# Attention's output projection as seven products over both token halves, with sums made by accumulating transfers

## The chip, the core and the metric

One core of a Trainium2 chip runs the kernel in one launch. TensorE (PE) multiplies, with its own queue for loading weights (PEld); VectorE (DVE), ScalarE (ACT) and GpSimd (POOL) work on elements; SyncE (SP) issues transfers, and so can POOL. Sixteen DMA engines carry the transfers of all queues. The metric is device time in microseconds; a run is compared by the median of several executions.

## The reference, cut to what matters

Two layers over 1024 tokens of width 1024, in fp32. Layer 0 mixes tokens by sliding-window attention (16 query heads, 4 key heads, blocks of 128, a sink per head), layer 1 by a gated recurrence; after each follows an MLP with squared ReLU (1024 to 4096 to 1024). The part that the change touches:

```python
def sliding_window_attention(h, positions, w_qkv, b_qkv, sinks, w_o):
    ...
    out = jnp.einsum('bnkgqs,bnskd->bnqkgd', probs.astype(vb.dtype), vb)
    return out.reshape(bsz, seq, Q_DIM) @ w_o

def sqrelu_mlp(h, w_up, w_down):
    return jnp.square(jax.nn.relu(h @ w_up)) @ w_down

    for layer in range(DEPTH):
        h = rmsnorm(x, mix_norm[layer])
        y = ...                       # attention in layer 0, recurrence in layer 1
        x = x + y
        h = rmsnorm(x, mlp_norm[layer])
        x = x + sqrelu_mlp(h, mlp_w_up[layer], mlp_w_down[layer])
```

## The kernel before, in words

All activations lie transposed: a tile is 128 channels by 512 tokens, so the width is 8 tiles (`KT`) and the tokens are two halves (`NH`). To keep fp32 accuracy, every operand of a matmul is split into a rounded high part and a rest (`split` for tokens, `weight_split` for weights: a cast on ACT, a subtraction on DVE), and `mm3` makes three matmuls of 128x512 for one product: high by high, high by low, low by high.

Most large products are already made by Strassen's method in Winograd's form: the operands are cut in two by two (inner channels and output channels of the weights; inner channels and token halves of the activations), and seven products with operand sums take the place of eight. The numbers 1 to 7 in the code name these products. In the MLPs, `begin` makes the operands that need the first token half only (1 and 2), `finish` the sums for 5, 3, 6, 7 and 4; `pair_first` starts the first two output tiles with products 1 and 2 while the sums are made, and `pair` does the rest.

Attention's output projection (`o_proj`) is plain: for each token half and each of 8 output tiles it sums 8 inner tiles. `attention` interleaves three stretches: `attend` of the first half beside `qkv` of the second, `attend` of the second half beside `o_proj` of the first, and `o_proj` of the second half beside `mlp_first`. `attend` works through 16 blocks a half (`attend_block`: scores, a masked maximum that includes the sink's column, exponentials, transposes; `values`: the product with the values).

The code states operations with a modelled cost in program order (`Schedule.add`). A planner (`forward`, `backward`, four passes) then lays them on the engines by readiness and due time, gives tiles their buffers, and fixes one order for each engine; PE takes them by their rank, the others by how late they may be. Each queue runs strictly in that order on the chip. All operations are issued from one helper, so nearly all rows of the profile have one line, and tiles are told apart by their tags: `a` (60 buffers of operands and activations), `t` (18), `m` (6), `wr` (raw weights), `wh` and `wl` (split weights), `p` and `q` (4 PSUM banks each), `c` (constants), `d` (kept in HBM).

A plain transfer is issued by SP (`dma`). `dma_sum` loads one tile on SP and adds a second onto it by an accumulating transfer on POOL's queue; before, the down projections' weights of product 5 are made so.

Of the kernel before, what the change touches and what calls it, by code (L numbers as in the profile page):

```python
# [139 lines left out]
SUM = 6000.0  # L140
# [242 lines left out]
class Net:  # L383
# [156 lines left out]
    def split(self, src, new=None):  # L540
        hi, lo = ((new or self.a)(F32R) for _ in range(2))
        self.copy(hi, src, TH, psum=False)
        self.tt("any", lo, src, hi.bitcast(F32), ALU.subtract)
        return hi, lo
# [46 lines left out]
    def lay_out(self):  # L591

        for v in (self.par, self.ones, self.ident, self.prev_mask, self.mean, self.eps, self.neg, *self.square[:1]):
            v.buf.handle()
# [52 lines left out]
    def gained(self, which, kt, hf):  # L647

        u = self.t()
        self.act(u, self.x[kt][hf], AF.Copy, scale=self.gain(which, kt))  # L650
        return u
# [7 lines left out]
    def begin(self, which):  # L659

        self.b, self.u = {k: [] for k in range(1, 8)}, []
        for kt in range(KT):
            u = self.gained(which, kt, 0)
            self.b[1 + kt // HK].append(self.split(u))
            self.u.append(self.keep(u))
            yield

    def finish(self, which, upper_first=False, keep=False):

        x, t, q01, q11 = self.b, [], [], []  # L670
        self.u3, self.u5 = [], []

        def stored(j):
            z = self.t()
            self.dma(z, self.u[j], 4 * P * TH)
            return z

        def lower():
            for j in range(HK):
                q01.append(self.gained(which, j, 1))  # L680
                t.append(stored(j))
                self.tt("any", t[j], q01[j], t[j], ALU.subtract)
                x[5].append(self.split(t[j]))
                if keep:
                    self.u5.append(self.keep(t[j]))
# [7 lines left out]

        for part in (upper, lower) if upper_first else (lower, upper):
            part()
        for j in range(HK):
            self.tt("any", t[j], q11[j], t[j], ALU.subtract)
            x[6].append(self.split(t[j]))
        for j in range(HK):
            self.tt("any", q01[j], q11[j], q01[j], ALU.subtract)  # L700
            x[7].append(self.split(q01[j]))
        self.u4 = []
        for j in range(HK):
            z = stored(j + HK)
            self.tt("any", z, z, t[j], ALU.subtract)
            x[4].append(self.split(z))
            if keep:
                self.u4.append(self.keep(z))
        return x

    def mlp_first(self, layer):
        self.layer, self.hid, self.y = layer, {}, {}
        yield from self.begin(2 + layer)
        if not layer:
            self.weigh(0)

    def mlp_second(self):
        self.first = [self.pair_first(m) for m in range(FIRSTS[self.layer])]
        x = self.finish(2 + self.layer, keep=True)
        if not self.layer:  # L720
            self.weigh(1)
# [42 lines left out]
    def inner_operands(self, own, kept, homes, stream=False):  # L764
# [15 lines left out]
        def split(name, z):  # L780
            y = self.split(z, new if homes else self.t)
# [16 lines left out]
        for j, c in enumerate((L, R) if homes else ()):  # L798
            hi, lo = part(own[j], R, "R")
            self.copy(hi, t[0][:, c], 2 * P, psum=False)  # L800
            self.tt("any", lo, t[0][:, c], hi.bitcast(F32), ALU.subtract, 2 * P)
# [176 lines left out]
    def mlp(self, cut):  # L978

        x = self.mlp_second()  # L980
        for m in range(MT // 2):
            if m == INNER[self.layer]:
                homes = iter(HOMES)
                self.quarters = {2: self.inner_operands(self.b[2], self.u[HK:], homes),
                                 3: self.inner_operands(self.b[3], self.u3, None),
# [4 lines left out]
            if self.layer and m == 1:  # L990
# [9 lines left out]
    def operands(self, name, p, T, S, held=False):  # L1000
# [11 lines left out]
        elif name == 5:  # L1012
# [3 lines left out]
            self.dma_sum(w, *(self.io["down"][self.layer, k, p, :, 1] for k in range(2)), 4 * P * TH)  # L1016
# [126 lines left out]
    def rope_tables(self):  # L1143
# [3 lines left out]
        late = self.x[KT // 2][0]  # L1147
        posf, ang = self.const((P, n)), self.const((P, n))
# [144 lines left out]
    def first_loads(self):  # L1293
# [4 lines left out]
        self.op("ACT", self.nc.scalar.dma_start, [self.par], [self.io["par"]], 100, self.par, self.io["par"], tail=3000.0)  # L1298
        for kt in range(KT):
# [64 lines left out]
    def attend(self, hf, out):  # L1364

        blocks = range(hf * BPH, hf * BPH + BPH)
        for gp in range(NG // 2):
# [3 lines left out]
            for e in range(2):  # L1371
                g = 2 * gp + e
                for j in range(2):
                    out[g, j] = self.a()
                for n in blocks[::4]:
# [4 lines left out]
                    self.values(g, n, parts, out)  # L1380

    def values(self, g, n, parts, out):
# [690 lines left out]
```

## Time and profile before

| | |
|---|---|
| median of 3 runs | 2018.03 us (2015.84 to 2018.79) |
| the profiled execution | 2015.63 us, span 2013.9 us |
| PE busy | 2003.4 us, granted clock 0.999 |
| DVE, ACT, POOL busy | 1801.6, 1308.0, 70.7 us |
| transfers | 521.25 MB, 75.1% of the DMA engines' time on SP's queue, 2.3% on POOL's |

The page is of one profiled execution, the sums of the prediction are made against its own time. Busy time of PE includes the overlap of pipelined matmuls, so a matmul's price is read from how many fit into a stretch, not from the duration of one. A line of the list of waits says which engine waited on which tile for whom, how long in all, how often, and the longest. A group of instructions shows engine, operation, result <- operands by tags, shapes, count, busy time and the mean of one, then the idle time ahead of them.

### The profile page before, as it was taken

To read this page: it belongs to the slowest core of one execution; us is meant where nothing else is said; L and a number is where in the kernel's file an instruction comes from. 1 tells how busy PE (TensorE), PEld (TensorE's weight loads), DVE (VectorE), ACT (ScalarE), POOL (GpSimd) and SP (SyncE) were. 2 spreads that over 40 slices of the span, in tenths; PEclk is the share of its full clock that TensorE was granted. 3 is DMA by queue.
4 is the path that set the end of the run, shared out by engine and by line. 5 is a ranking of instruction groups with operands and counts; after the bars stand their busy time and mean duration, and the time that the engine had idled before them with its cause. 6 is when DMAs were issued, how large, how long until landed. Compare 5 with 4: busy or idle time off the path is not lost. (4 is left out here: it accounts for less than half of the span.)

```text
span 2013.9 us, 40072 instructions
## 1 busy us (share of the span) xinstructions
PE 2003.4 (99%) x13820; PEld 1700.7 (84%) x13820; DVE 1801.6 (89%) x3636; ACT 1308.0 (65%) x2746; POOL 70.7 (4%) x161
## 2 busy tenths in 40 slices
PE   9999999999999999999999999999999999999998
PEld 8887888899998888888888888888889998888887
DVE  8879879899898979889999999999999998987985
ACT  7677976677675444667666666666767667444573
POOL 2000000000001000000000000000000001100000
PEclk9999999999999999999999999999999999999999
DMA  7857388688799967755888889989789789986812
GB/s 251 265 165 242 123 290 278 219 278 283 267 297 332 342 225 241 250 174 186 284 286 288 285 284 316 319 296 317 256 290 306 262 291 294 350 294 219 272 53 84
DMA packets 290875, 521.25 MB, mean 259 GB/s; under 512 B 33648, under 2 KB 42224, under 8 KB 290672
## 3 DMA queue, kind: packets, MB, share of 16 engines
q1 hardware_dynamic: 285920, 510.28, 75.1%
q0 software_dynamic: 4608, 8.39, 2.3%
q8 instruction: 109, 1.79, 0.4%
q14 instruction: 94, 0.77, 0.1%
q10 hardware_dynamic: 144, 0.02, 0.0%
HBM read 407.84 MB, written 110.72 MB: 257 GB/s over the span
## 5 line engine op out<-in xcount | busy, mean ns | idle before, releaser
L437 PE MATMUL p<-a,wh 128*128 128x512 f32 (+1 forms) x3152 | 881.5, 364 | 0.1
L437 PEld LDWEIGHTS p<-a,wh 128*128 128x128 f32 x3152 | 560.4, 189 | 90.2 <-issue 0.8
L437 PE MATMUL q<-a,wh 128*128 128x512 f32 x2020 | 625.4, 390 | 0.1
L437 PE MATMUL p<-a,wl 128*128 128x512 f32 (+1 forms) x1576 | 567.2, 362 | 0.3 <-DVE wl L437 0.3
L437 PEld LDWEIGHTS q<-a,wh 128*128 128x128 f32 x2020 | 374.6, 188 | 74.2 <-ACT t L437 0.5
L437 PE MATMUL q<-a,wl 128*128 128x512 f32 x1008 | 391.5, 390 | 0.0
L437 PEld LDWEIGHTS p<-a,wl 128*128 128x128 f32 x1576 | 296.2, 189 | 45.2 <-DVE wl L437 0.8
L437 ACT CAST wh<-m 128x512 fp32r<-128x512 f32 (+1 forms) x354 | 212.7, 605 | 177.0 <-PE q L437 90.8
L437 ACT CAST wh<-wr 128x512 fp32r<-128x512 f32 (+1 forms) x324 | 193.8, 601 | 136.8 <-PE p L437 83.9
L437 DVE TENSOR_TENSOR wl<-m,wh 128x512 fp32r<-128x512 f32 (+1 forms) x354 | 235.0, 669 | 40.6 <-ACT wh L437 34.1
L437 DVE TENSOR_TENSOR t<-t,t 128x512 f32<-128x512 f32 (+3 forms) x404 | 230.8, 594 | 13.3 <-DMA t<-d 5.2
L437 DVE TENSOR_TENSOR wl<-wr,wh 128x512 fp32r<-128x512 f32 (+1 forms) x324 | 214.8, 666 | 27.7 <-ACT wh L437 25.0
L437 DVE TENSOR_TENSOR a<-t,a 128x512 fp32r<-128x512 f32 (+2 forms) x321 | 211.0, 676 | 25.3 <-ACT a L437 13.3
L437 PEld LDWEIGHTS q<-a,wl 128*128 128x128 f32 x1008 | 189.3, 188 | 39.2 <-DVE wl L437 0.2
L437 ACT ACTIVATE t<-t 128x512 f32<-128x512 f32 x288 | 179.9, 631 | 51.1 <-DVE t L437 45.2
L437 ACT CAST a<-t 128x512 fp32r<-128x512 f32 (+1 forms) x241 | 143.0, 607 | 58.6 <-DMA t<-d 35.3
L437 DVE TENSOR_TENSOR t<-t,p 128x256 f32<-128x256 f32 x288 | 116.0, 416 | 14.9 <-PE p L437 11.4
L437 ACT COPY t<-q 128x512 f32<-128x512 f32 (+2 forms) x254 | 111.7, 442 | 22.3 <-PE q L437 12.4
L437 DVE TENSOR_TENSOR a<-a,a 128x512 fp32r<-128x512 f32 (+2 forms) x151 | 101.1, 681 | 9.3 <-ACT a L437 6.5
L437 ACT CAST a<-a 128x512 fp32r<-128x512 f32 x136 | 83.0, 619 | 37.8 <-DVE a L437 31.6
L437 DVE TENSOR_TENSOR m<-wr,wr 128x512 f32<-128x512 f32 (+1 forms) x152 | 97.7, 643 | 0.7 <-DMA wr<-in_up 0.3
L437 PE MATMUL p<-t,wh 128*128 128x256 f32 x480 | 91.4, 283 | 0.0
(131 smaller groups left out, 2183.2 us busy)
## 6 DMA issues: line engine op xcount, KB each, us to landing
t<-d SPq DMA_DIRECT2D x592, 256.0 KB
a<-d SPq DMA_DIRECT2D x350, 256.0 KB
d<-t SPq DMA_DIRECT2D x318, 256.0 KB
wr<-in_up SPq DMA_DIRECT2D x172, 256.0 KB
wr<-in_down SPq DMA_DIRECT2D x160, 256.0 KB
wr<-in_win SPq DMA_DIRECT2D x68, 256.0 KB
d<-a SPq DMA_DIRECT2D x64, 256.0 KB
wr<-in_wqkv SPq DMA_DIRECT2D x48, 256.0 KB
```

The source lines that it names most:

```text
L437: fn(*[place(a) for a in args], **{k: place(v) for k, v in kw.items()})
```

## The change

`o_proj` is one generator over both token halves. Its seven products run in the order 1, 2, 5, 3, 6, 7, 4: 1, 2 and 5 beside the second half of attention, the rest behind it. Products 1, 2, 5, 6, 7 use the four `p` banks, 3 and 4 the four `q` banks. What the weights need as sums is made by accumulating transfers (`proj_weight`: product 3's weight is one load and three accumulations onto it), and so are most sums of token tiles (`dma_add`) and half of the residual additions. To let transfers add only, some tiles are carried with a negative sign: `values` writes half of attention's output times -1, `gained` has a negative gain (`self.minus`), and `split` can split -1 times its source. In the MLPs' `finish`, the sums for products 7 and 4 become accumulating transfers too (8 in each MLP); the recurrence's keep the vector engine. `weigh` (sums of squares of the residual for the norm, and its store) is called behind the third pair of layer 0's MLP and no longer in `mlp_first` and `mlp_second`. `attend` of the first half now runs beside 18 of the 24 steps of `qkv`, the rest comes beside the second half.

```diff
-    def dma_sum(self, out, x, y, nbytes):
-        self.dma(out, x, nbytes)
-        self.op("Pool", self.nc.gpsimd.dma_start, [out], [out, y], 1200.0, out, y, accum_op=ALU.add, tail=SUM)
+    def dma_add(self, out, y):
+        self.op("Pool", self.nc.gpsimd.dma_start, [out], [out, y], 900.0, out, y, accum_op=ALU.add, tail=SUM)
+
+    def dma_sum(self, out, x, *more):
+        self.dma(out, x, 4 * P * TH)
+        for y in more:
+            self.dma_add(out, y)
...
     def finish(self, which, upper_first=False, keep=False):
...
+        def add(z, y):
+            if keep:
+                self.dma_add(z, y)
+            else:
+                if not isinstance(y, View) or y.buf.tag[0] == "d":
+                    d, y = y, self.t()
+                    self.dma(y, d, 4 * P * TH)
+                self.tt("any", z, z, y, ALU.add)
...
         for j in range(HK):
-            self.tt("any", q01[j], q11[j], q01[j], ALU.subtract)
-            x[7].append(self.split(q01[j]))
+            add(n01[j], q11[j])
+            x[7].append(self.split(n01[j]))
         for j in range(HK):
-            z = stored(j + HK)
-            self.tt("any", z, z, t[j], ALU.subtract)
-            x[4].append(self.split(z))
+            add(t[j], self.u[j + HK])
+            x[4].append(self.split(t[j], sign=-1.0))
...
-    def o_proj(self, hf, out):
-
-        a = [self.split(out[g, j]) for g in range(NG) for j in range(2)]
-        for m in range(KT):
-            w = self.blocks(self.weight(self.io["wo"][m]))
-            x = self.t()
-            self.dma(x, self.io["x"][hf, m], 4 * P * TH)
-            ps = self.psum()
-            for kt in range(KT):
-                self.mm3(ps, w[kt], a[kt], kt == 0, kt == KT - 1)
-            self.x[m][hf] = self.a()
-            self.tt("DVE", self.x[m][hf], ps, x, ALU.add)
-            yield
+    def proj_weight(self, name, p, kept):
+        a = lambda i, k: self.io["wo"][k, p, :, i]
+        self.s.lead = LEAD
+        if name in (1, 2, 4):
+            z = self.raw(a(*{1: (0, 0), 2: (0, 1), 4: (1, 1)}[name]))
+        elif name == 5:
+            z = kept[p] = self.a()
+            self.dma_sum(z, a(1, 0), a(1, 1))
+        elif name == 6:
+            z = kept[p]
+            self.dma_add(z, a(0, 0))
+        else:
+            z = self.a()
+            self.dma_sum(z, a(0, 0), a(1, 0), *((a(1, 1), a(0, 1)) if name == 3 else ()))
+        w = self.weight_split(z)
+        self.s.lead = 0
+        return w
+
+    def o_proj(self, out, b):
+        kept, ready, p1, p5, later, x = {}, {}, [], [], [], {k: [] for k in range(1, 8)}
+        order = [(name, p) for name in (1, 2, 5, 3, 6, 7, 4) for p in range(HK)]
+        main = [self.psum() for _ in range(HK)]
+        b00, n10 = b
...
+        yield from product(2, main, False)
+        for m in range(HK):
+            z = self.x[m][0] = residual(m, 0)
+            self.tt("DVE", z, main[m], z, ALU.add)
+            self.copy(main[m], p1[m], psum=False)
+        n01 = [out[1][p // 2, p % 2] for p in range(HK)]
+        t = b00
+        for p in range(HK):
+            self.dma_add(t[p], n01[p])
+            x[5].append(self.split(t[p]))
+        yield from product(5, main, False)
...
+        b11 = [out[1][2 + p // 2, p % 2] for p in range(HK)]
+        for p in range(HK):
+            if p < HK // 2:
+                self.dma_add(t[p], b11[p])
+            else:
+                self.tt("DVE", t[p], t[p], b11[p], ALU.add)
+            x[6].append(self.split(t[p], sign=-1.0))
+            x[3].append(self.split(b11[p]))
+        for p in range(HK):
+            self.dma_add(t[p], n10[p])
+            x[4].append(self.split(t[p]))
+            self.dma_add(b11[p], n01[p])
+            x[7].append(self.split(b11[p]))
+        side = [self.psum("q") for _ in range(HK)]
+        yield from product(3, side, True)
+        yield from product(6, main, False)
...
+        yield from product(4, side, True)
+        for m in range(HK):
+            z = self.x[m + HK][0] = later[m]
+            self.tt("DVE", z, z, side[m], ALU.subtract)
+        yield
...
-        interleave(self.attend(0, out[0]), self.qkv(1, *h[1]), 16, 24)
-        interleave(self.attend(1, out[1]), self.o_proj(0, out[0]), 24, 8)
-        interleave(self.o_proj(1, out[1]), self.mlp_first(layer), 4, 8)
+        rest = self.qkv(1, *h[1])
+        for k, _ in enumerate(self.attend(0, out[0])):
+            for _ in range((k + 1) * 18 // 16 - k * 18 // 16):
+                next(rest)
+        tiles = [[out[0][2 * k + p // 2, p % 2] for p in range(HK)] for k in range(2)]
+        proj, first = self.o_proj(out, tiles), self.mlp_first(layer)
+        side = chain(rest, proj)
+        left = 6 + 13
+        for k, _ in enumerate(self.attend(1, out[1])):
+            for _ in range((k + 1) * left // 16 - k * left // 16):
+                next(side)
...
```

POOL's queue beside the second half of attention held only the sinks' columns before (`m` are attention's score tiles, `c` the sinks):

```order
L437 TENSOR_SCALAR m708_2922<-c5152_772 128x4
L437 TENSOR_SCALAR m716_3018<-c5152_772 128x4
L437 TENSOR_SCALAR m728_3050<-c5152_772 128x4
L437 TENSOR_SCALAR m745_3113<-c5152_772 128x4
L437 TENSOR_SCALAR m753_3180<-c5152_772 128x4
L437 TENSOR_SCALAR m761_3238<-c5152_772 128x4
```

In the changed program accumulations stand between them (`a<-in_wo` are weights, `a<-a` token tiles; `a781` is product 3's first weight):

```order
L438 DMA a781_2655<-in_wo 128x512
L438 DMA a264_1546<-a527_2916 128x512
L438 DMA a265_1552<-a528_2921 128x512
L438 DMA a781_2655<-in_wo 128x512
L438 TENSOR_SCALAR m713_2994<-c5253_778 128x4
L438 DMA a721_2550<-in_wo 128x512
L438 DMA a825_2883<-in_wo 128x512
L438 DMA a828_2891<-in_wo 128x512
L438 TENSOR_SCALAR m728_3038<-c5253_778 128x4
L438 TENSOR_SCALAR m751_3067<-c5253_778 128x4
```

The second row for `a781` waits there for the landing of the first, and the columns behind it with it; 28 accumulations and the last ten columns share the queue up to attention's end.

On PE the projection's end and the MLP's begin stood so before (`p936` is the last output tile of the second token half, `a824` an operand of the MLP from the first half):

```order
L437 MATMUL p936_4138<-a812_3610,wh933_4041 128x512
L437 MATMUL p936_4138<-a813_3619,wh933_4041 128x512
L437 MATMUL p936_4138<-a812_3610,wl934_4060 128x512
L437 MATMUL q944_4204<-a824_3217,wh939_4071 128x512
L437 MATMUL q944_4204<-a825_3284,wh939_4071 128x512
```

Now (`q818` and `q821` are the first and the last bank of product 4, `q913` and `p914` the MLP's first products 1 and 2; the `a892` of product 2 comes from the result in `q818`):

```order
L438 MATMUL q818_3545<-a814_3796,wl890_3959 128x512
...
L438 MATMUL q821_3671<-a814_3796,wl890_3959 128x512
L438 MATMUL q913_4077<-a832_3581,wh908_3949 128x512
...
L438 MATMUL q913_4077<-a871_3606,wl909_3968 128x512
L438 MATMUL p914_4115<-a892_4079,wh911_3979 128x512
L438 MATMUL p914_4115<-a893_4089,wh911_3979 128x512
...
L438 MATMUL p914_4115<-a904_4120,wl912_3989 128x512
```

From the last matmul into `q818` to the first that reads `a892` there are 21 others; before, the first token half of the residual was complete long ahead of this place.

More of the change, by code (lines that the diff above doesn't have):

```diff
@@ L1 @@
 import heapq
+from itertools import chain
 from contextlib import ExitStack
@@ L139 @@
 LOAD, STORE = 4200.0,3200.0
-SUM = 6000.0
+SUM = 6400.0
 HALF = {"ACT": 125.0, "DVE": 105.0}
@@ L538, in blocks, with split @@
         return [(hi[:, c : c + P], lo[:, c : c + P]) for hi, lo in w for c in range(0, TH, P)]
-    def split(self, src, new=None):
+    def split(self, src, new=None, sign=1.0):
         hi, lo = ((new or self.a)(F32R) for _ in range(2))
-        self.copy(hi, src, TH, psum=False)
-        self.tt("any", lo, src, hi.bitcast(F32), ALU.subtract)
+        if sign > 0:
+            self.copy(hi, src, TH, psum=False)
+            self.tt("any", lo, src, hi.bitcast(F32), ALU.subtract)
+        else:
+            self.act(hi, src, AF.Copy, scale=sign)
+            self.stt(lo, src, sign, hi.bitcast(F32), ALU.mult, ALU.subtract)
         return hi, lo
@@ L591, in lay_out @@
     def lay_out(self):
-        for v in (self.par, self.ones, self.ident, self.prev_mask, self.mean, self.eps, self.neg, *self.square[:1]):
+        for v in (self.par, self.minus, self.ones, self.ident, self.prev_mask, self.mean, self.eps, self.neg, *self.square[:1]):
             v.buf.handle()
@@ L662, in begin @@
         for kt in range(KT):
-            u = self.gained(which, kt, 0)
-            self.b[1 + kt // HK].append(self.split(u))
+            sign = 1.0 if kt < HK else -1.0
+            u = self.gained(which, kt, 0, sign)
+            self.b[1 + kt // HK].append(self.split(u, sign=sign))
             self.u.append(self.keep(u))
@@ L780, in split @@
         def split(name, z):
-            y = self.split(z, new if homes else self.t)
+            y = self.split(z, new if homes else self.t, sign)
             x[name] = [tuple(v[:, c] for v in y) for c in (L, R)] if homes and not stream else self.put_by(y)
@@ L1015, in operands @@
             w = self.t(tag="m")
-            self.dma_sum(w, *(self.io["down"][self.layer, k, p, :, 1] for k in range(2)), 4 * P * TH)
+            self.dma_sum(w, *(self.io["down"][self.layer, k, p, :, 1] for k in range(2)))
         elif name == 6:
@@ L1147, in rope_tables @@
         late = self.x[KT // 2][0]
+        self.op("DVE", self.nc.vector.tensor_scalar, [self.minus], [self.par, late], 100, self.minus, self.par, -1.0, None, ALU.mult)
         posf, ang = self.const((P, n)), self.const((P, n))
@@ L1374, in attend @@
                     out[g, j] = self.a()
+                sign = 1.0 if hf == gp else -1.0
                 for n in blocks[::4]:
@@ L1392, in values @@
             for j in range(2):
-                self.copy(out[g, j][:, b * 2 * P : b * 2 * P + 2 * P].only(n + 2 * b), po[b][:, j], 2 * P)
+                self.act(out[g, j][:, b * 2 * P : b * 2 * P + 2 * P].only(n + 2 * b), po[b][:, j], AF.Copy, 2 * P, scale=sign)
     def attend_block(self, g, n, stacks):
@@ L1458, in attention @@
         h.append(self.scaled(layer, 1))
-        interleave(self.attend(0, out[0]), self.qkv(1, *h[1]), 16, 24)
-        interleave(self.attend(1, out[1]), self.o_proj(0, out[0]), 24, 8)
-        interleave(self.o_proj(1, out[1]), self.mlp_first(layer), 4, 8)
+        rest = self.qkv(1, *h[1])
[9 more added lines that the diff above has]
+                next(side)
+        for k in range(14):
+            next(proj)
+            if k % 3 == 2:
+                next(first)
+        run(proj)
+        run(first)
     def hgrn_constants(self):
```

102 lines of the change are left out of this document (75 added, 27 removed).

## The prediction, made before the changed kernel ran

> **What bounds the kernel now.** I read the page's busy shares first, then what PE waited for, then the stretches around the output projection.
>
> ```profile
> span 2013.9 us, 40072 instructions
> PE 2003.4 (99%) x13820; PEld 1700.7 (84%) x13820; DVE 1801.6 (89%) x3636; ACT 1308.0 (65%) x2746; POOL 70.7 (4%) x161
> ...
> PE p L437 <- DVE t L437: 1.1, 1, 1.1
> PE q L437 <- DVE sm L437: 1.0, 1, 1.0
> PE p L437 <- ACT a L437: 0.8, 1, 0.8
> PE q L437 <- DVE t L437: 0.5, 2, 0.3
> PE p L437 <- DVE wl L437: 0.3, 1, 0.3
> PE q L437 <- ACT m L437: 0.2, 1, 0.2
> PE q L437 <- ACT wh L437: 0.2, 1, 0.2
> ```
>
> PE is busy for 2003.4 of 2013.9 us, and all waits that the list of waits gives it come to 4.1 us. So a matmul taken out is worth its own time, as long as PE's next operand stands ready earlier by as much. What one matmul is worth shows where PE does nothing else; these are a row of the chain of waits, and by stretches (columns: stretch, its length, then busy us and count of PE, PEld, DVE, ACT and POOL, the granted clock, the DMA engines' share, GB/s):
>
> ```profile
> 1868.82 43.52 PE p L437 x192
> ...
> 130.00:210.00 80.00, 79.98 (x485) 64.90 (x482) 69.35 (x134) 64.11 (x208) 6.31 (x14) 1.00 0.71 232
> 210.00:250.00 40.00, 40.00 (x261) 31.85 (x261) 35.85 (x72) 35.77 (x124) 0.90 (x4) 1.00 0.21 68
> 250.00:304.00 54.00, 54.00 (x281) 43.92 (x276) 43.41 (x72) 39.89 (x72) 0.00 (x0) 1.00 0.87 286
> 304.00:360.00 56.00, 56.00 (x278) 46.12 (x278) 51.89 (x101) 37.17 (x66) 0.00 (x0) 1.00 0.81 269
> 587.00:680.00 93.00, 92.98 (x457) 78.70 (x457) 84.48 (x149) 52.17 (x95) 13.99 (x16) 1.00 1.04 334
> ```
>
> 192 matmuls of 128x512 take 43.52 us, 0.2267 us each, at a granted clock of 1.00. On PE's timeline the second half of attention begins at 183 us and ends at 252 us, and the first matmul of the MLP starts at 304 us:
>
> ```profile
> 182.94 0.28 PE L437 MATMUL q<-a,a 128*128 128x256 f32 x1
> ...
> 248.72 3.67 PE L437 MATMUL q<-t,a 128*64 128x256 f32 x32
> ...
> 304.04 0.62 PE L437 MATMUL q<-a,wh 128*128 128x512 f32 x2
> ...
> 290.00:350.00 60.00, 60.00 (x296) 49.46 (x295) 59.27 (x114) 44.08 (x80) 0.00 (x0) 1.00 0.82 270
> ```
>
> The projection lies from 183 to 304 us, beside and behind that half of attention; PE has no gap there. The last row, a stretch again, has DVE busy for 59.27 of 60 us, and PE still does not wait: the planner can run DVE almost full beside PE.
>
> **Removed.** The projection was 2 token halves x 8 output tiles x 8 inner tiles x 3 = 384 matmuls; seven products of 4 x 4 x 3 make 336. In the built order only the 128x512 matmuls change in number (p banks -144, q banks +96), so 48 go: 48 x 0.2267 = 10.88 us off PE. This term is certain as far as nothing new holds PE up.
>
> **Added on DVE and ACT.** Counted over the whole order, DVE has 3 instructions more and ACT 19 more. DVE's 3 are +19 in the projection (more splits and more results read from the banks) against -16 in the two MLPs, whose sums for products 7 and 4 become transfers. One costs:
>
> ```profile
> L437 DVE TENSOR_TENSOR a<-t,a 128x512 fp32r<-128x512 f32 x16 | 10.8, 687 | 3.3 <-ACT a L437 3.3
> L437 DVE TENSOR_TENSOR a<-p,t 128x512 f32<-128x512 f32 x15 | 10.3, 686 | 6.3 <-PE p L437 6.3
> L437 ACT CAST a<-t 128x512 fp32r<-128x512 f32 x19 | 11.4, 616 | 2.6 <-DVE t L437 2.6
> L437 ACT ACTIVATE t<-a,c 128x512 f32<-128x512 f32 x14 | 10.1, 725 | 2.1 <-DVE a L437 2.1
> L437 ACT COPY a<-q 128x256 f32<-128x256 f32 x32 | 10.4, 371 | 8.7 <-PE q L437 8.4
> ```
>
> 19 x 0.68 = 12.9 us more DVE work from 130 to 304 us, where it is busy for 69.35 + 35.85 + 43.41 = 148.6 of 174 us. The sums of squares of the first token half (7 additions, 4.8 us) leave this stretch: both halves are now taken in the MLP. That makes 156.7 of 163.1 us (174 less the 10.88), 96%. Covered, it costs nothing, as at 98.8% from 290 to 350 us. Uncovered, it costs at most what a DVE that gets no fuller than from 210 to 250 us (90%) would need beyond the stretch: 156.7 / 0.9 - 163.1 = 11.0 us. I take 0.9 us, near the row at 98.8%, which is the same engine with the same kinds of work. ACT, at 139.8 of 174 us, gets about 11 us and keeps 12 free: nothing. From 304 to 360 us the 7 additions come in and 8 of the MLP's sums (5.5 us) go: nothing; the results of the squares are wanted only at the end of the MLP.
>
> **Added on POOL and the DMA engines.** 62 accumulating transfers: 46 in the projection (24 for weights, 14 between token tiles, 8 that bring the residual) and 8 in each MLP; SP issues 24 transfers fewer. What one costs shows where the kernel before used them (the two queue rows of 1690 to 1720 us, with the DMA engines full; then POOL's issues and their landing):
>
> ```profile
> q1 hardware_dynamic: 4706, 8.56, 76.8%
> q0 software_dynamic: 864, 1.58, 28.6%
> ...
> L437 POOL DMA_DIRECT2D m<-in_down x32: 862/862/1032, 587.9 to 1760.4; - x32
> DMA to landing us min/median/max: 5.9/6.8/8.0
> ```
>
> 8.56 MB are 32.7 plain transfers of 256 KB in 0.768 x 30 us, 0.71 us each; 1.58 MB are 6.0 accumulating ones in 0.286 x 30 us, 1.42 us each: one takes the engines as long as two plain ones. POOL needs 0.86 us to issue and the sum stands 6.8 us after the issue.
>
> In the order 28 of the 46 stand beside the second half of attention, which keeps PE for some 70 us (180 matmuls of 128x512 now, 40.8 us, and attention's own): 28 x 1.42 = 39.8 us, and about 39 transfers of SP x 0.71 = 27.7 us: 67 of 70 us. The engines are as full there as from 587 to 680 us (share 1.04), where PE worked 92.98 of 93 us. Before, 210 to 250 us stood nearly empty (0.21).
>
> The tightest operand is product 6's first. Its accumulation needs a tile that attention finishes just before: two evacuations 2 x 0.37, landing 6.8, split 0.72: 8.3 us. In the order 36 matmuls of 128x512 (8.2 us), 16 of 128x256 (half: 1.8) and 12 transposes stand between: 10 us and more. With the slowest landing, 8.0, it is 9.5 us: still in time, with 0.5 us and the transposes left. Bounds of the cost: 0 and, if the landing took twice its median, 13.6 + 1.5 - 10 = 5.1 us; I take 1.2 us for this and the other operands that come by such transfers, the trace's own spread of landing (8.0 - 6.8).
>
> **At the seam to the MLP** the last four residual tiles now come from the last product. Between the end of the first bank (9 matmuls ahead of the projection's end) and the first matmul that reads its operand stand 21 matmuls, 4.76 us; the chain is DVE 0.69, ACT 0.73, ACT 0.62: 2.04 us plus three hand-overs. The fourth tile follows at ACT's pace, 3 x 1.34 later, 6.06 us, and is wanted at 4.76 + 3 x 0.68 = 6.80 us; its low half, 0.69 us later, at 7.03 us. Cost 0 to 1 us; I take 0.3. If another ACT instruction comes between, 0.6 us more each.
>
> **The sum.** The profiled execution took 2015.63 us (span 2013.9). 2015.63 - 10.88 + 0.9 + 1.2 + 0.3 = 2007.15 us. The median of the runs shown, 2018.03, lies 2.40 above that execution: 2009.5 us is the forecast, 0.42% faster.
>
> **Rivals.**
>
> *The DMA engines get too full.* For it: 67 of 70 us by the price above, and the share of 0.87 from 250 to 304 us. Against it: 9 of the 12 accumulations of product 3 and those of product 7 stand in the order some 20 us of matmuls ahead of their use, so a backlog falls on them first. If a backlog of one landing and a half (10 us) reaches the operands of products 5 and 6 with their 2 us of room, 8 us go: 2017.5 us, no change. Of the Trainium skill, "DMA: Bandwidth & Descriptors" (Issuing engines are not separate DMA queues) says that transfers issued by different engines run on the same 16 DMA engines and interleave. The trace agrees (76.8% + 28.6%): POOL's queue adds no room.
>
> *POOL's queue holds attention up, and the kernel gets slower.* Attention's sink column is written by POOL, a block at a time; here the first and the last two of the kernel before, which waited for their tile only:
>
> ```profile
> 84.40 0.42 POOL L437 TENSOR_SCALAR m<-c 128x4 f32<-128x4 f32 x1 [28.94 <-PE q L437]
> ...
> 221.12 0.22 POOL L437 TENSOR_SCALAR m<-c 128x4 f32<-128x4 f32 x1 [5.73 <-PE q L437]
> 224.50 0.22 POOL L437 TENSOR_SCALAR m<-c 128x4 f32<-128x4 f32 x1 [3.16 <-DVE wl L437]
> ```
>
> Now the last ten stand behind accumulations of which many wait for the landing of the one before into the same tile. Behind a sink column wait DVE's row maximum, the exponentials, the transposes and then PE, whose order is fixed. Ten landings later by the spread of 1.2 us are 12 us, and two held by another 2 us are 16: 2018.03 - 10.88 + 16 = 2023 us. It decides once the new waits pass 10.88 + 4 = 14.9 us. Against it: POOL is nearly idle (0.90 of 40 us before), six m tiles let a column be written some blocks ahead of its use, and the planner places POOL's work too. The Trainium skill, "SBUF — State Buffer" (SBUF: two separate sides), has a rule against this change: while DVE runs an operation that takes both ports (an fp32 copy within SBUF), GpSimd cannot write the descriptors of its transfers. It would be one way to these late landings. The trace does not show it so far: 862 to 1032 ns per issue while DVE was busy 84.48 of 93 us.
>
> *DVE becomes the bound of the projection.* For it: 96% where it was 85%. Against it: the row at 98.8%. It costs the 11.0 us above in place of 0.9: 2019.6 us, no change.
>
> That the matmuls aren't saved is excluded by the count in the order.
>
> **How the numbers follow.** Forecast 0.70, full DMA engines 0.12, POOL's queue 0.07, DVE 0.11. A measurement of this kernel tells 0.2% (4 us) from no change. The forecast's case is faster; of the DMA and the DVE case a third each is faster (the loss only half as large), 0.02 slower, the rest the same: 0.70 + 0.08 = 0.78 faster; 0.07 + 0.02 = 0.09 slower; 0.13 the same. Without any new wait a run like the quickest would take 2015.63 - 10.88 = 2004.75 us; the range goes from 2004.5 to 2018.2, into the cases of DMA and DVE, and leaves out POOL's. The forecast's own is 2004.5 to 2013.
>
> **What would show it.** Right: the first matmul of the MLP starts about 8.5 us earlier (304 us before), and PE's idle time grows by 2 to 3 us, at product 6 and at the seam. Wrong: PE waiting for a DMA on tiles a between 200 and 260 us (full engines), for DVE sm or ACT m behind POOL rows that waited for a landing (POOL's queue), for DVE with DVE at 9.9 of 10 (DVE); or a lower clock, or a longer matmul than 0.227 us, which nothing here leads to expect.

## The result, and the profile after

The changed kernel takes 2040.05 us (median of 5, 2037.56 to 2041.69), the kernel before on the same chip 2018.02 us (5 runs): a ratio of 1.0111, with a 95% interval of 1.0096 to 1.0125. It is slower by 22 us, where 2009.5 us, 8.5 less than before, had been forecast. The profiled execution has a span of 2038.3 us. Its page and the list of what PE waited for (in all, times, longest, in us):

```profile
span 2038.3 us, 40062 instructions
PE 2001.9 (98%) x13772; PEld 1698.9 (83%) x13772; DVE 1803.7 (88%) x3639; ACT 1316.2 (65%) x2765; POOL 125.7 (6%) x223
...
PE q L438 <- ACT t L438: 10.7, 4, 5.0
PE q L438 <- DMA a<-d: 8.7, 2, 7.5
PE p L438 <- ACT a L438: 4.5, 1, 4.5
PE q L438 <- ACT a L438: 1.6, 1, 1.6
...
PE q L438 <- DVE sm L438: 1.0, 1, 1.0
```

The 48 matmuls are gone (13820 to 13772), but PE's busy time fell by only 1.5 us, from 2003.4 to 2001.9, where 10.9 were to go; and PE is idle for 36.4 us of the span instead of 10.5. So the 24.4 us that the span grew are 25.9 us of new idle time less 1.5 us. The other 9.4 us are matmuls that took longer: the mean granted clock is 0.993, 0.999 before. The stretches show where (busy us and count of PE, PEld, DVE, ACT, POOL, then clock, DMA share, GB/s):

```profile
200.00:220.00 20.00, 12.10 (x80) 9.27 (x76) 11.32 (x22) 11.20 (x41) 7.78 (x10) 0.88 1.04 260
220.00:240.00 20.00, 19.21 (x114) 15.40 (x115) 14.25 (x29) 14.92 (x54) 9.30 (x12) 0.87 0.91 218
240.00:260.00 20.00, 18.77 (x118) 14.67 (x116) 18.10 (x35) 17.67 (x59) 6.15 (x7) 1.00 1.08 261
260.00:280.00 20.00, 16.69 (x85) 12.67 (x86) 14.60 (x24) 13.79 (x27) 6.98 (x8) 0.91 0.85 186
...
340.00:360.00 20.00, 17.43 (x65) 14.19 (x66) 15.42 (x25) 14.81 (x27) 0.00 (x0) 0.83 0.69 235
```

The DMA engines reach 1.04 and 1.08, in a piece of the program that stood at 0.21 before, from 210 to 250 us. On PE's timeline there are four long gaps, and the chain of waits gives for each what ended last (start, length, what):

```profile
218.76 0.79 PE L438 MATMUL q<-a,a 128*128 128x256 f32 x2 [7.46 <-DMA a<-d]
263.31 2.08 PE L438 MATMUL p<-a,wh 128*128 128x512 f32 x4 [4.54 <-ACT a L438]
342.57 1.22 PE L438 MATMUL q<-a,wh 128*128 128x512 f32 x2 [5.01 <-ACT t L438]
1437.35 1.22 PE L438 MATMUL q<-a,wh 128*128 128x512 f32 x2 [4.48 <-ACT t L438]
```

```profile
191.22 6.76 DMA d<-t
...
208.61 12.14 DMA a<-d
...
241.31 10.64 DMA a<-in_wo
...
252.51 0.50 POOL a L438
...
253.58 9.03 DMA a<-a
...
262.63 0.64 ACT a L438
...
332.86 5.88 DMA d<-t
...
1425.58 8.98 DMA d<-t
```

The first gap is attention's own: the query stacks that are loaded back from HBM (`a<-d`) took 12.14 us to come, behind a store that had taken 6.76. The second is a projection operand, product 6's: an accumulation of weights (10.64 us), then one between token tiles (9.03 us), then its split. The two have no operand in common; what joins them in the chain is POOL's queue, in which the token tiles' accumulation was issued behind two onto weights, the first of them held until the 10.64 us were over. The third and the fourth are at the start of the two MLPs, where ACT stands in its order before an instruction whose `t` buffer is still being stored (5.88 and 8.98 us; a store in the chain of the kernel before takes 3.10 us). Only the second waits directly for a tile that an accumulating transfer makes. The others are plain transfers that came late.

### The profile page after: what moved, and what is told of

It is laid out like the page before. It is cut to its first block, busy times and chain, and to the rows that moved or that the text cites. A ratio compares the mean times of both kernels' runs of the same rounds, so it can differ in the third digit from the quotient of the medians.

```text
span 2038.3 us, 40062 instructions
## 1 busy us (share of the span) xinstructions
PE 2001.9 (98%) x13772; PEld 1698.9 (83%) x13772; DVE 1803.7 (88%) x3639; ACT 1316.2 (65%) x2765; POOL 125.7 (6%) x223
## 4 chain that ended last, share of the span: by engine, by line
PE 89%; DMA 4%; DVE 4%; ACT 2%; issue 1%; SPq 0%; POOL 0%; DVEq 0%; ACTq 0%; POOLq 0%
PE p L438 48%; PE q L438 41%; DMA d<-t 2%; DVE t L438 2%; ACT t L438 1%; DMA a<-d 1%; DVE m L438 1%; DVE wl L438 1%; DMA a<-in_wo 1%; DMA a<-a 0%; ACT a L438 0%; DVE a L438 0%; ACT wh L438 0%; SPq L438 0%; DMA a<-in_x 0%
## 5 line engine op out<-in xcount | busy, mean ns | idle before, releaser
L438 PE MATMUL p<-a,wh 128*128 128x512 f32 (+1 forms) x3056 | 852.1, 363 | 4.8 <-ACT a L438 4.5
L438 PE MATMUL q<-a,wh 128*128 128x512 f32 x2084 | 650.1, 393 | 12.5 <-ACT t L438 10.4
L438 PEld LDWEIGHTS p<-a,wh 128*128 128x128 f32 x3056 | 544.3, 189 | 90.8 <-ACT a L438 5.2
L438 PE MATMUL p<-a,wl 128*128 128x512 f32 (+1 forms) x1528 | 549.1, 362 | 0.4 <-DVE wl L438 0.4
L438 PEld LDWEIGHTS q<-a,wh 128*128 128x128 f32 x2084 | 388.4, 189 | 92.5 <-ACT t L438 12.1
L438 PE MATMUL q<-a,wl 128*128 128x512 f32 x1040 | 405.1, 391 | 0.0
L438 DVE TENSOR_TENSOR wl<-wr,wh 128x512 fp32r<-128x512 f32 (+1 forms) x304 | 200.3, 664 | 34.1 <-ACT wh L438 29.1
L438 DVE TENSOR_TENSOR t<-t,t 128x512 f32<-128x512 f32 (+3 forms) x382 | 215.8, 586 | 12.5 <-DMA t<-d 5.8
L438 DVE TENSOR_TENSOR a<-t,a 128x512 fp32r<-128x512 f32 (+1 forms) x261 | 173.6, 684 | 17.9 <-PE q L438 8.5
L438 ACT CAST a<-t 128x512 fp32r<-128x512 f32 x181 | 109.3, 617 | 43.5 <-DMA t<-d 26.4
L438 ACT COPY t<-q 128x512 f32<-128x512 f32 (+2 forms) x254 | 111.7, 442 | 25.6 <-PE q L438 16.4
```

Source lines behind the costliest of these rows:

```text
L438: fn(*[place(a) for a in args], **{k: place(v) for k, v in kw.items()})
```

## The experiments

All times are medians. The kernel before took 2018.02 us beside the changed one, and 2015.97, 2016.48, 2016.30 and 2016.40 us in the four later sessions, so what an edit is worth is told by its cost against the kernel before of its own session: the changed kernel costs 22.0 us. The intervals of the ratios leave 1.8 to 3.4 us open in each. Where an edit changes operations, the planner lays out all orders anew, so such a run shows the edit together with its new orders. Theory 1 is that the accumulating transfers fill the DMA engines.

### The MLPs' sums back on VectorE

```diff
-            if keep:
-                self.dma_add(z, y)
-            else:
+            if True:
                 if not isinstance(y, View) or y.buf.tag[0] == "d":
```

> The changed kernel, with the MLPs' sums for products 7 and 4 on DVE again (16 additions and 8 loads for 16 accumulating transfers). In the changed kernel PE stood still for 5.0 us at 337 us and for about as long in the second MLP, each time until an ACT operation on a tile t, and the clock was 0.83 in the 20 us behind the first. Theory 1, the DMA engines are too full and stores and loads land late: both gaps and the slow clock behind them go, 2 x (5 + 3.4) = 17 us, about 2023 us (2020 to 2028). Rival, the gaps come from DVE or from the plan and only move: 2035 us or more.

Measured: 2026.54 us, ratio 1.0046 (1.0029 to 1.0063). That is a cost of 10.6 us against before, 11.4 less than the change's (13.5 by the two medians alone, which is the figure that later expectations use). The two MLP gaps are gone; the two in attention stay (waits: `DMA a<-d` 8.0, `ACT a` 5.0 us). The prediction had costed these 16 transfers at nothing.

### Plain transfers in the place of the accumulating ones

```diff
-[out, y], 900.0, out, y, accum_op=ALU.add, tail=SUM)
+[out, y], 900.0, out, y, tail=SUM)
```

> The changed kernel with every accumulating transfer on POOL replaced by a plain one of the same size into the same tile; it leaves the additions out, so that it computes something else, with the same instructions, queues and waits. Theory 1 (full DMA engines): 94 transfers cost 0.71 us of the engines in place of 1.42, 67 us less in all, PE's waits fall from 30 us to under 10 and the clock stays above 0.997: 2006 to 2018 us. Rival, POOL's queue (its order and its 0.86 us an issue hold attention and the sums up): POOL issues the same rows in the same order, the waits stay: 2033 us or more.

Measured: 2010.74 us, ratio 0.9972 (0.996 to 0.9984). The additions are left out; the orders, the issues on POOL and all that waits for them stay. The edit reaches 94 transfers, the 62 of the change and the 32 for the down projections' weights that the kernel before has too. The kernel now does nearly what had been forecast. The queue rows from 170 to 345 us, first of the changed kernel, then of this one (packets, MB, share of the 16 engines):

```profile
q1 hardware_dynamic: 16947, 29.29, 49.2%
q0 software_dynamic: 7776, 14.16, 47.0%
```

```profile
q1 hardware_dynamic: 19657, 34.21, 57.2%
q0 software_dynamic: 4320, 14.16, 24.0%
```

The same 14.16 MB, 54 transfers of 256 KB, take 47.0% of 175 us as accumulations, 1.52 us each, and 24.0% as plain ones, 0.78 us each. PE waits 2.0 us for `a<-d` instead of 8.7, and in the same 175 us 5 MB more pass on SP's queue. The rival that POOL's queue holds attention up through the sink columns is not borne out: from 100 to 420 us PE has no wait for `DVE sm` or `ACT m` before, after or here (the 1.0 us for `DVE sm` in each list lies behind 2000 us). But this run does not separate full engines from waits in POOL's queue altogether, since a plain transfer also lands earlier (median 5.5 us for the weights, 7.7 as accumulations) and frees the queue earlier: POOL waits 17.0 us for landings of weights from 170 to 270 us here, 30.4 in the changed kernel.

### The planner told of longer transfers

```diff
-LOAD, STORE = 4200.0,3200.0
-SUM = 6400.0
+LOAD, STORE = 5200.0,6200.0
+SUM = 8600.0
```

and 1400 instead of 900 for an accumulating issue.

> The changed kernel, with longer transfers in the planner's model alone: loads 5.2 us (4.2), stores 6.2 (3.2), accumulations 8.6 and 1.4 on POOL (6.4 and 0.9), as they were seen near the gaps (stores 6 to 7 us, one group of loads 12 us, sums 8.6). Same transfers in number. Theory 1 in its strict form (there is no room in the engines): gaps remain, 2025 us or more. Rival, the plan (the order was made for transfers that are quicker than the chip's, and there is room to be early): the gaps go, 2005 to 2018 us.

Measured: 2037.47 us, ratio 1.0102 (1.0087 to 1.0117). That is 21.5 us of cost, 0.5 less than the change, which the intervals do not tell from nothing. In the profiled execution (2032.61 us) the long gaps break up into more short ones, of at most 2.3 us. So it is not an order made with too short transfer times: the engines hold 1.07 to 1.11 from 200 to 280 us whichever way they are laid out.

### The shift of qkv alone

In the kernel before, 18 instead of 24 steps of `qkv` beside the first half of attention, the other six beside the second.

> The kernel before with one thing of the change alone: 18 of the 24 steps of the second half's projection of queries, keys and values beside the first half of attention, and 6 beside the second. The longest stall of the changed kernel, 8.7 us at 211 to 221 us, waits for the loads of attention's second stack of queries, which this shift brings later. Theory 1: without accumulations the shift costs little, within 4 us of 2018. Rival, the shift makes the stall: 2018 + 8.7 and 5 us of slower clock, 2028 to 2034 us.

Measured: 2016.92 us, ratio 1.0005 (0.9996 to 1.0014), no gap. The shift costs nothing by itself.

### The MLPs' transfers alone

> The changed kernel with the output projection of before (plain, eight products) and only the MLPs' 16 accumulating transfers kept. Taking these 16 out of the whole change gave back 13.5 us. Theory 1 (an accumulating transfer takes the DMA engines twice as long as a plain one, and the stretch in which the MLP begins is already at 0.8 to 0.9 of its engines): each MLP has its gap of 4 to 5 us, with ACT behind stores that land late, and a clock loss behind it, whatever the projection does: 2016 + 9 to 14, 2025 to 2030 us. Rival (the backlog that the MLP meets is left over from the projection's 46 accumulations): the first MLP has no gap and only the second keeps one, 2016 + 4 to 7, 2020 to 2023 us.

Measured: 2022.18 us, ratio 1.0031 (1.0018 to 1.0044): 5.7 us of cost, at the upper end of what the rival said. The first MLP has no gap; in the second PE waits twice for ACT, 1.81 and 1.09 us, with a clock of 0.90 and 0.93 in the stretches of 10 us that hold them. That the rest of the loss is a backlog of the projection looked confirmed; the last run shows that this cannot be all of it.

### Token sums and residual off the transfers

On the kernel with the MLPs' sums on VectorE; here one of the four token sums, and one of the two residual additions:

```diff
-            self.dma_add(b11[p], n01[p])
+            self.tt("any", b11[p], b11[p], n01[p], ALU.add)
...
-            z = self.a()
-            self.copy(z, main[m])
-            self.dma_add(z, self.io["x"][1, m])
+            z = residual(m, 1)
+            self.tt("DVE", z, main[m], z, ALU.add)
```

> Strassen's projection with the 14 token sums and the 8 residual additions on VectorE or ScalarE's neighbours instead of accumulating transfers (8 plain loads more, some 26 VectorE operations of 0.69 us more, 17.8 us), the MLPs' sums on VectorE too; the 24 accumulations for weights stay. It stands beside the kernel with only the MLPs' sums moved, 2026.5 us. Theory 1 (full DMA engines): 24 accumulations of 1.42 us instead of 46 take 31 us off the engines and 11 for the loads go on, in some 110 us; the waits shrink from 14 us to 3 to 6 and the clock stays up: 2009 to 2017 us. Rival 2 (VectorE is the bound, 96% of the projection by the estimate before): 17.8 us more do not fit, 2026.5 + 10 to 18, 2036 to 2044 us, with PE waiting for VectorE at 9.9 of 10.

Measured: 2015.71 us, ratio 0.9998 (0.9989 to 1.0007): 0.8 us below the kernel before, 11.4 better than with the transfers, within what theory 1 gave. One wait of 1.9 us for `a<-d` is left.

### Fewer weight sums as well

Product 6 comes ahead of product 3, whose weight is then product 6's sum and one accumulation:

```diff
-        order = ... for name in (1, 2, 5, 3, 6, 7, 4) ...
+        order = ... for name in (1, 2, 5, 6, 3, 7, 4) ...
-            self.dma_sum(z, a(0, 0), a(1, 0), *((a(1, 1), a(0, 1)) if name == 3 else ()))
+        elif name == 3:
+            z = kept[p]
+            self.dma_add(z, a(0, 1))
...
+            self.dma_sum(z, a(0, 0), a(1, 0))
```

> As the kernel with token sums and residual on VectorE, and the weight sums made from one another: product 3's weight is one accumulation onto product 6's sum, with product 6 ahead of product 3, so 16 accumulations and 20 loads for weights instead of 24 and 24. Theory 1: another 8 x 1.42 + 4 x 0.71 = 14 us off the DMA engines; waits for DMA of at most 2 us and a clock of 0.998 or more: 2006 to 2013 us, faster than before. If the chain of accumulations into one tile is what is late (each waits for the landing of the one before) rather than the engines' load: product 3's chain is now as long as product 6's plus one, so the waits stay, 2012 to 2020 us. VectorE as the bound: 2036 to 2044 us as in the run beside it.

Measured: 2015.10 us, ratio 0.9993 (0.9984 to 1.0002). The list of waits has none for a DMA any more, as theory 1 said, but the kernel gained only 0.6 us, which the intervals do not tell from nothing, and its time lies above theory 1's range. It is not faster than before, and the waits that the case of the chain of accumulations named are not there either. Its stretches show what has taken over:

```profile
260.00:280.00 20.00, 20.00 (x89) 16.54 (x89) 19.98 (x33) 10.47 (x18) 0.00 (x0) 1.00 0.27 86
280.00:300.00 20.00, 20.00 (x90) 16.56 (x89) 19.77 (x34) 15.26 (x27) 0.00 (x0) 1.00 0.76 258
300.00:320.00 20.00, 18.54 (x78) 14.12 (x77) 19.86 (x34) 15.47 (x29) 0.00 (x0) 1.00 0.88 300
```

From 260 us on DVE is busy for 19.77 to 19.98 of 20 us, PE still full; then, when the MLP begins at 300 us, PE waits for operands one after the other. The DMA engines are at 0.27 and 0.76 ahead of that.

### No accumulation at all

The 16 weight sums on VectorE too.

> Strassen's projection with every sum on VectorE: no accumulating transfer in it or in the MLPs; 16 weight sums of 0.69 us (11 us) more on VectorE than in the kernel of the run before it, 16 plain loads in place of 16 accumulations. Theory 1 alone: no wait for DMA is left, 2016 - 10.9 + 0 to 4 = 2005 to 2009 us. If VectorE has no room for 29 us more in the projection than the changed kernel gave it, PE waits for it: 5 to 20 us more than the run before it, 2012 to 2030 us, with waits for DVE or for tiles that DVE frees. It shows what the accumulating transfers are worth when nothing is wrong with them.

Measured: 2020.58 us, ratio 1.0020 (1.0010 to 1.0030), 5.5 us worse than with 16 accumulations, as the second of the two cases said:

```profile
300.00:320.00 20.00, 16.49 (x56) 10.07 (x55) 20.00 (x35) 14.50 (x25) 0.00 (x0) 0.94 0.96 312
320.00:340.00 20.00, 18.14 (x69) 13.89 (x69) 17.50 (x29) 16.13 (x30) 0.00 (x0) 0.89 0.60 195
```

20.00 of 20 us for DVE, and PE does 56 matmuls where a full stretch of 20 us holds 90; no single wait of PE there is longer than 1.19 us. So the accumulating transfers are worth something: VectorE has no room for all the sums of this projection.

### Fewer weight sums alone

> Beside the kernel with the MLPs' sums on VectorE (2026.5 us): product 3's weight is one accumulation onto product 6's sum and product 6 comes ahead of product 3: 16 accumulations and 20 loads for weights instead of 24 and 24; the 14 token sums and 8 residual accumulations stay as transfers. It splits the gain of 11 us between weight sums and token sums. Load of the DMA engines as the cause: 8 x 1.42 + 4 x 0.71 = 14 us less of them, half of what taking the token and residual sums off gave (22 x 1.42 less 8 x 0.71 = 26 us): 2026.5 - 4 to 7, 2019 to 2023 us. If the waits come from the token sums' own landing (an operand that attention has just finished, then 7 us of transfer) and not from the load, product 6's operand is wanted even earlier with the new order: 2026 to 2032 us.

Measured: 2013.92 us, ratio 0.9988 (0.998 to 0.9997): 2.4 us below the kernel before, 13.0 better than with 24 weight accumulations, where 4 to 7 had been expected of the load. PE still waits 4.0 us for `a<-d`, in four parts, where it was 8.0. The same edit gave 0.6 us where the token and residual sums were off the transfers. So what 14 us of the DMA engines are worth depends on what else is on them. That product 6 comes earlier is part of the edit in both, and no run takes it apart from the fewer transfers.

### Residual by transfers, token sums on VectorE

> As the kernel with 16 accumulations for weights and the token sums on VectorE (2015.1 us), but the 8 residual additions are accumulating transfers again: 12 VectorE operations (8 us) fewer, 8 ScalarE copies and accumulations more, from some 265 to 300 us, where the DMA engines were at 0.27. Theory (with the load gone from the engines, VectorE at 20.00 of 20 us until the MLP begins is what costs the rest: PE 18.54 of 20 us there): the gap at the MLP's start closes, 2015.1 - 3 to 6, 2009 to 2012 us, faster than before. Rival (the loss against 2016 - 10.9 is spread over the kernel, or lies with the transfers that are left): 2013 to 2017 us.

Measured: 2008.00 us, ratio 0.9957 (0.9944 to 0.997). The 8 accumulations lie from 265 to 300 us, where the engines were at 0.27 and 0.76, and take 8 instructions off DVE just ahead of the MLP (x3677 to x3669 on the pages): 8.3 us below the kernel before, 6.9 better than with them on VectorE, a little more than the 3 to 6 expected.

### The late token sums by transfers too

The sums for products 7 and 4 are accumulations as in the change; those for 5 and 6 stay on VectorE.

> As the kernel with the residual by transfers, and the token sums of products 7 and 4 (8 of the 14), which are wanted 30 us after their inputs stand, are accumulating transfers too; those of products 5 and 6 stay on VectorE. 32 accumulations in the projection, none of them on an operand that PE wants within 15 us. Theory (an accumulation is free where its operand is not wanted soon and the engines have room; VectorE is the other bound): 8 VectorE operations (5.5 us) fewer, 2006 to 2011 us. If the engines from 210 to 250 us are what counts, where the weights' sums and these lie together, 8 x 1.42 = 11 us more of them there bring waits back: 2013 to 2019 us.

Measured: 2007.41 us, ratio 0.9953 (0.9941 to 0.9965). It computes all that the reference does, and is faster than both kernels: 8.9 us below the one before, 30.9 below the changed one. 32 accumulations are left where the change has 62 (the edit to product 3's weight needs 8 fewer), and no long gap remains. The 0.6 us to the kernel before it are not told from nothing:

```profile
span 2003.9 us, 40057 instructions
PE 1992.3 (99%) x13772; PEld 1692.3 (84%) x13772; DVE 1810.3 (90%) x3661; ACT 1315.3 (66%) x2765; POOL 98.8 (5%) x193
...
200.00:220.00 20.00, 20.00 (x143) 15.55 (x138) 18.25 (x38) 18.13 (x69) 6.96 (x11) 1.00 0.94 266
...
260.00:280.00 20.00, 20.00 (x90) 16.57 (x89) 16.69 (x27) 13.74 (x24) 5.60 (x7) 1.00 1.03 240
```

The engines are at 1.03 here too, from 260 to 280 us, and PE waits for nothing then.

Against the kernel with fewer weight sums alone, beside which it was run (2013.92 us), this one differs only in the six token sums of products 5 and 6. Moving them to VectorE is worth 6.5 us. PE's largest wait there was not for these sums but for attention's plain reloads, the 4.0 us for `a<-d`, with a slower clock, where the row of the same stretch above has PE full:

```profile
200.00:220.00 20.00, 15.98 (x86) 12.57 (x82) 12.88 (x27) 12.80 (x46) 6.14 (x8) 0.86 1.01 287
```

### The same with the MLPs' transfers put back

> The kernel with 32 well-placed accumulations (2007.4 us) with the MLPs' 16 accumulating transfers put back. In the kernel before, these 16 alone cost 5.7 us; taken out of the changed kernel they gave 13.5. Theory (the two share the engines: half of the 13.5 was the projection's backlog, the rest is the MLPs' own): 5 to 7 us of cost, 2012 to 2015 us, with PE waiting for ScalarE on tiles whose stores land late. Rival (VectorE was the bound of the first MLP's start, at 19.97 of 20 us, and the transfers relieve it): 2003 to 2008 us. If the 13.5 us were the MLPs' own wherever they stand: 2018 to 2021 us.

Measured: 2023.87 us, ratio 1.0034 (1.0021 to 1.0048): 7.5 us above the kernel before, 16.4 above the kernel without them, more than any of the three cases had said. The third, that the loss is the MLPs' own, is nearest. PE's timeline at the first MLP, then the stretches of the second, some 1,100 us behind attention's output projection:

```profile
326.92 1.22 PE L438 MATMUL q<-a,wh 128*128 128x512 f32 x2 [4.96 <-ACT t L438]
327.93 0.63 PE L438 MATMUL q<-a,wl 128*128 128x512 f32 x1
328.36 1.05 PE L438 MATMUL q<-a,wh 128*128 128x512 f32 x2
329.21 0.63 PE L438 MATMUL q<-a,wl 128*128 128x512 f32 x1
329.64 1.05 PE L438 MATMUL q<-a,wh 128*128 128x512 f32 x2
330.49 0.56 PE L438 MATMUL q<-a,wl 128*128 128x512 f32 x1
330.89 0.63 PE L438 MATMUL q<-a,wh 128*128 128x512 f32 x2
331.36 0.40 PE L438 MATMUL q<-a,wl 128*128 128x512 f32 x1
```

```profile
1390.00:1400.00 10.00, 10.00 (x46) 8.27 (x45) 10.00 (x18) 9.12 (x17) 2.28 (x3) 1.00 1.07 253
1400.00:1410.00 10.00, 10.00 (x46) 8.26 (x45) 9.20 (x16) 7.21 (x15) 3.56 (x4) 1.00 1.04 347
1410.00:1420.00 10.00, 4.86 (x17) 3.58 (x16) 5.54 (x10) 5.98 (x12) 0.00 (x0) 0.81 1.10 313
```

In the twenty microseconds ahead of the gap and in it the engines are at 1.04 to 1.10; the chain of waits has this there, with PE behind ACT:

```profile
1409.22 7.23 DMA d<-t
...
1416.55 0.59 ACT t L438
```

In the kernel without the transfers the same place has PE full:

```profile
1400.00:1410.00 10.00, 10.00 (x45) 8.04 (x45) 10.00 (x18) 9.91 (x20) 0.00 (x0) 1.00 0.75 245
```

The waits of 4.96 and 5.14 us and the slow matmuls behind them make some 7 us in the first MLP and 8 in the second; ahead of the first PE also waits 2.61 us for DVE. In the second MLP no backlog of the projection can be left. In the first it stays open: the 32 accumulations of the projection are there too, and the chain runs through one of the MLP's own accumulations (6.71 us) into a store (7.09 us). Why the same 16 cost only 5.7 us beside the plain projection is not settled: there the engines were as full, and PE did not wait in the first MLP:

```profile
300.00:320.00 20.00, 20.00 (x90) 16.57 (x89) 19.11 (x32) 16.69 (x31) 3.46 (x4) 1.00 1.08 329
```

So full engines alone do not make the gap; I take it that the order decides which transfer is late, but no run takes that apart.

## Why the prediction was wrong

**Removed** was right: 10.88 us. In the best kernel PE is busy for 1992.3 us, 11.1 less than before, and its 2007.41 us are 8.9 below the 2016.3 beside it, so 2.0 us of the saving went to small stalls; the prediction had allowed 2.4.

**Added on POOL and the DMA engines** is the step that failed. Its price was right: 1.42 us of the engines for an accumulation was taken, 1.52 measured. Its sum was borne out too: 67 of 70 us had been expected beside the second half of attention, and from 183 to 253 us the two queues hold 43.7 and 54.7% of the engines, 69 of 70 us. What failed is the conclusion, that engines as full as from 587 to 680 us do no harm because PE had no gap there. A share tells how full the engines are, not what is late. Beside attention the queue also carries stores and reloads of the query stacks, and the plain transfers came late: 6.76 us for a store, 12.14 for a load. The prediction timed only the accumulations' own operands, with 0.5 us of room and the transposes at product 6, and asked of no other transfer what it costs if it takes twice as long. At product 6 PE did wait, 4.54 us, within the bound of 5.1, but not by the landing of twice its median that gave the bound: the landing took 9.03 us where 6.8 had been taken, and ahead of it the accumulation stood in POOL's queue behind another landing of 10.64 us, a wait that the sum does not have. Taken at 1.2 us (bounds 0 to 5.1), this step cost 19.5 us, the distance from the kernel without the MLPs' transfers (+10.6) to the best one (-8.9).

**The MLPs' 16 transfers** appear in the same step's count and nowhere in its sum; that part only booked the VectorE work they remove. They cost 11.4 us in this kernel, by taking them out, and 16.4 us in the best one, by putting them in.

**The rival of full DMA engines** named the right mechanism and gave it 0.12: three of the four long gaps wait for plain transfers on SP's queue, and they go when POOL's transfers are plain. Its sign came, PE waiting for a DMA on `a` between 200 and 260 us. Its size was wrong, 8 us against 19.5 in the projection and 30.9 with the MLPs, because it too let the delay reach only the operands of products 5 and 6.

**The rival of POOL's queue** had the wrong path: no sink column held PE up. Its mechanism, work on POOL that stands behind the wait for a landing, did come, at product 6's operand; how much of the 4.54 us it made and how much the landings themselves no run tells. POOL's issues also got longer, 1270 ns in the mean for the weight sums where 862 to 1032 had stood:

```profile
L438 POOL DMA_DIRECT2D m<-in_down x32 | 27.6, 864 | 693.5 <-DVE wl L438 573.6 <-DVE a L438 56.8 <-ACT wh L438 31.0
L438 POOL DMA_DIRECT2D a<-in_wo x24 | 24.0, 1270 | 46.6 <-DMA a<-in_wo 30.4 <-DVE sm L438 7.5 <-PE q L438 5.4
```

The down projections' accumulations keep 864 ns. What lengthens the others was not tried.

**VectorE as the bound** was not what made the change slower: DVE has 11.32 to 15.42 of 20 us in the stretches with the gaps. But it stood right behind: with the sums moved there, PE lacks operands at the start of the MLP, 6.9 us for the residual's 8 instructions and 5.5 us for 16 more. The row at 98.8% was a poor witness: 59.27 of 60 us went without a wait before, 59.61 of 60 from 260 to 320 us go with waits in the kernel with 16 accumulations. Such a share does not tell whether work has piled up.

**The lower clock**, which the prediction said nothing led to expect, took 9.4 us. Most of it follows from the four long gaps, as the last section shows: the three of 4.48 to 5.01 us were worth 5.9 to 7.7 us each.

## What to carry to other kernels

Here an accumulating transfer of 256 KB took the DMA engines as long as two plain ones (1.52 and 0.78 us), so count the sums you move there in engine time by stage, and where the share comes near 1.0 ask which plain transfers with little room share that stage, not only when the sum itself is wanted, and what stands behind it in the issuing queue. Put on such transfers what is not wanted soon and lies where the engines have room (the best kernel's rule was 15 us; no run tries another figure), and leave urgent sums to the vector engine (six of them were worth 6.5 us): 32 transfers, well placed, made the kernel 0.47% faster, all 62 made it 1.1% slower. When two resources are both near full, work has to be divided between them by stage; either extreme was slower than the kernel before.

## What the hardware showed that was not expected

**A gap costs more than its length.** After the gap of 4.96 us quoted above, nine matmuls take from 326.92 to 330.89 us, 0.44 each, and then they follow at 0.23 again. At 0.2267 us they would take 2.04 us, so 1.9 are lost. In the changed kernel the same count gives 1.4 us behind the second gap (6 matmuls in 2.73 us), 2.7 behind the third (13 in 5.68 us) and 1.6 behind the fourth (8 in 3.37 us); behind the first the clock is 0.50 and 0.51 in the 5.0 us for which PE is busy from 215 to 225 us, 2.5 us lost. Together these are 8.2 of the 9.4 us by which PE's work got longer. The Trainium skill, "TensorE: Matmul & The Clock Gate" (Part 1: The HAM clock gate), says that an idle window of about 3.4 us halves TensorE's clock until it has been busy for about as long; that half speed lasts some 4 us behind 4.96 us of idleness agrees. A shorter wait did it too, which that rule does not lead to expect. In the kernel with the token sums on VectorE, attention's matmuls and those of the projection wait for 1.85 us, and the 512-wide ones go slowly for 4 us, with a clock of 0.77 in the stretch behind (timeline, then the stretch):

```profile
212.62 0.47 PE L438 MATMUL q<-a,a 128*128 128x256 f32 x2 [1.85 <-DMA a<-d]
...
215.03 0.63 PE L438 MATMUL p<-a,wl 128*128 128x512 f32 x1
215.45 0.63 PE L438 MATMUL p<-a,wh 128*128 128x512 f32 x1
...
218.15 0.40 PE L438 MATMUL p<-a,wh 128*128 128x512 f32 x1
```

```profile
215.00:220.00 5.00, 5.00 (x26) 4.28 (x24) 3.40 (x7) 3.01 (x10) 2.12 (x5) 0.77 1.02 368
```

So a wait of 2 us for one late load can cost 4. The wait of 1.81 us in the second MLP of the kernel with the MLPs' transfers alone did the same: nine matmuls from 1417.90 to 1421.55 us take 0.41 each. In the kernel without accumulations no wait is longer than 1.19 us, but they follow one another, and the clock falls to 0.77, 0.84 and 0.70 in the stretches of 5 us from 315 to 330 us. Why these did, and the 1.58 us wait of the changed kernel at 313.78 us left the clock at 1.00, is not settled.

**The loss is not additive.** The edit that takes 14 us of work off the DMA engines gave 13.0 us with 22 other accumulations present, and 0.6 without them, although the engines stand at 1.00 and 1.07 from 200 to 240 us there too.
